# Three reorderings in a streaming-encoder block: the first weights and the residual's loads, the lag of the transposes, and where the recurrences' steps end a round

## The chip, the core and the metric

The kernel runs on one core of one Trainium2 chip. A core has a matrix engine (TensorE, "PE" in the profile), a vector engine (VectorE, DVE), a scalar engine that evaluates functions (ScalarE, ACT), GpSimd (POOL), and a queue on SyncE (SP) that issues the loads and stores in this kernel. Each engine runs its own instruction stream in order and waits on semaphores for the others. Matrix products accumulate in PSUM, of which this kernel uses eight banks (128 partitions by 512 fp32 numbers); everything else lives in SBUF.

The metric is the device time of one execution, in microseconds (us), as the median over several runs. The profile is of one execution.

## The reference

The reference is one layer of a streaming encoder on x of 256 tokens by 2048 features, in fp32, with a fixed memory of 256 tokens:

```python
x = x + 0.5 * swiglu(rms_norm(x, ffn1_norm), w_up1, w_down1)      # D_FF = 5632
h = rms_norm(x, mix_norm)
q, f, v, g, x_b, gate_b, gates = split(h @ w_in)
y_a = hgrn2(q, f, v) -> rms_norm -> * silu(g)                     # 8 heads of 128
y_b = causal conv(4) on x_b -> RG-LRU scan -> * gelu(gate_b)      # 8 blocks of 128
gt = sigmoid(gates + b_gate)
x = x + (gt[0] * (y_a @ w_branch_a) + gt[1] * (y_b @ w_branch_b)) @ w_out
x = x + cross_attention(rms_norm(x), rms_norm(mem))               # 4 heads
x = x + 0.5 * swiglu(rms_norm(x, ffn2_norm), w_up2, w_down2)
return rms_norm(x, final_norm)
```

In HGRN2 the state of a head is updated by S = diag(f) S + (1 - f) v^T; the kernel computes it through decayed scores between tokens. In RG-LRU the gates r and i are sigmoids of small block-diagonal products of the convolved input, and a linear recurrence runs over the tokens.

## The kernel before

**Weights and splits.** All weights are streamed once, in pieces of 1 MB (128 partitions x 2048). Each large fp32 product is computed as three products of a shorter type: every operand is split into h (an ACT copy, L147) and l = raw - h (a DVE subtraction, L148), and PE computes h*xh, l*xh and h*xl (`three`, L424 to L426). So ahead of each piece stand a load on SP, an ACT instruction and a DVE instruction. `weights` (L191) hands out the next piece and keeps `ahead` at two pieces: it issues the load and the split of a later piece whenever one is taken. `raw`, `h` and `l` have three buffers each.

**FFN pieces.** The two FFNs have 22 groups of 256 hidden features (gate and up) with four pieces each, and 11 blocks of the down projection with four pieces each. Twelve of the groups are "fast": two-by-two blocks multiplied with seven products in place of eight, at 42 matmuls of 256 columns a piece; their weights need sums `td` on DVE and their inputs sums `xs` (L413). A piece of an "up" group or of the down projection is 24 matmuls of 512 columns. `ffn_order` (L43) writes out the order of the pieces in Python: it spreads the fast pieces evenly from index `begin` on, and puts in the pieces of two down blocks at a time once four groups are ready for them. It counts a group ready from `seen`, the number of groups that had ended one step earlier. FFN1 has `begin` 7, FFN2 has 3.

**From a group to its transpose.** When a group's fourth piece is through, `activate` computes hid = (up * rstd) * silu(gate * rstd), 128 tokens at a time: sg on ACT (L449), hid on DVE (L450). For a fast group the sums `c` and `ev` (L496 to L504) come first. `hid` has two buffers. PE must then transpose hid (four transposes, L458, in `turn`), and ACT and DVE split the result into `hidop` (L462, L463), which the down projection reads. To keep PE from waiting for hid, `turn` is put on a list `late` with a count of 2, and `tick`, called after each piece, issues it when the count has run out, so two pieces later in the program. The tile scheduler then sets the final order on each engine, near the program's.

**The head.** FFN1 begins while nothing is loaded. For its first pieces the order of SP, ACT and DVE is the program's own, under a `manual_schedule` that closes when the fifth piece (i = 4) has been prepared. `head` is a list of things to do just before the load of piece i: the transposed x in four parts (`head_x`, pieces 0 to 3), then `head_residual` (L555, ahead of piece 4): the second part of `vt`, which holds the identity for the transposes, and the eight loads of x in token layout, with the squares for the RMS norm (`junk`, L350), and then `head_fast` (L562) for the sums of the fast pieces, ahead of pieces 5 and 6. The norm's scale rstd needs all squares; its square root (L357) and the first Silu (L449) each need their own activation table on ACT.

**The mixer's rounds.** In the mixer each unit (one or four weight pieces of a projection) is followed by `pump(2)` (L621), which takes two steps of the generators in `side`: `hgrn(hf)` (L701) or `lru(hf)` (L787), each for half of the heads. A step ends at a `yield`. In this way the recurrences' small matmuls, the ACT and the DVE work run between the projections' matmuls. The steps touched here:

- At the end of the scores in `hgrn`, four products go to PSUM and ACT copies them to `S` (L762). The next step multiplies `S` by v for two heads (L771, L772) and squares the result on ACT (`osq`, L775); the one after it sums the squares with `ones` on PE (L780) and takes the square root.
- `lru` convolves one block of 128 channels after another (xc: L803 on ACT, three L805 on DVE), with a `yield` behind the first and third of those three, and then has two products with the gates' weights (L811) and two sigmoids (L812). So the products of one block stand in the same step as the beginning of the next block's convolution.

Of the kernel before, what the change touches and what calls it, by code (L numbers as in the profile page):

```python
# [10 lines left out]
ACT = mybir.ActivationFunctionType  # L11
ALU = mybir.AluOpType

P = 128
# [29 lines left out]
def ffn_order(fast, begin):  # L44

    left = {"fast": fast, "up": NU - fast}
    begun = {"fast": None, "up": None}  # L50
    out, ended, down = [], [], []
    names = count()
    blocks = seen = 0

    def step(kind):
        if begun[kind] is None:
            begun[kind] = [next(names), 0]
            left[kind] -= 1
        g, i = begun[kind]
        out.append((kind, g, i))  # L60
        begun[kind] = [g, i + 1]
        if i == 3:
            ended.append(g)
            begun[kind] = None

    total = 4 * (NU + NB)
    while len(out) < total:
        fasts = sum(e[0] == "fast" for e in out)
        more = left["fast"] or begun["fast"]
        if more and fasts * (total - begin - 9) < 4 * fast * (len(out) - begin):  # L70
            step("fast")
            continue
        if not down and not begun["up"]:
            ready = seen // 2 - blocks
            if ready >= 2 or (ready and not left["up"] and not more):
                n = min(2, ready)
                down = [("down", blocks, n, c, b) for c in range(4) for b in range(blocks, blocks + n)]
                blocks += n
        seen = len(ended)
        if down:  # L80
            out.append(down.pop(0))
        elif left["up"] or begun["up"]:
            step("up")
        elif more:
            step("fast")
    number = {g: i for i, g in enumerate(ended)}
    return [(e[0], number[e[1]], e[2]) if e[0] != "down" else e for e in out]
# [3 lines left out]
def block_kernel(ctx: ExitStack, tc: tile.TileContext, xT, xin, memT, vec, gfin, bgate, lruw, wu1, wd1, win, wv,  # L91
# [60 lines left out]


    plan, ahead = [], []
    orders = {"ffn1": ffn_order(FAST, 7), "ffn2": ffn_order(FAST, 3)}

    def plan_ffn(name, wu, wd):
        for e in orders[name]:
# [25 lines left out]
            plan_rows(name, w, g)  # L184
    plan_ffn("ffn2", wu2, wd2)

    head = []
    planned = count()
    in_turn = ExitStack()

    def weights(*key):  # L191
        while plan and len(ahead) < 2:
            i = next(planned)
            k, src, fast = plan.pop(0)
            if i == 0:
                in_turn.enter_context(tc.manual_schedule(engines={sp.engine, act.engine, dve.engine}))
            inner = head[i]() if i < len(head) else None
            ahead.append((k, prepare(src, fast, 4 if i < 4 else 1, inner)))
            if i == 4:
                in_turn.close()  # L200
        k, w = ahead.pop(0)
        assert k == key, (k, key)
        return w
# [229 lines left out]
    def ffn(name, pairs, sq, then, begin=()):  # L433
# [7 lines left out]
        def activate(g, gate, up):  # L441

            nonlocal rstd
            if rstd is None:
                rstd = sq.rstd_tokens()
            hid = scoped["hd"].tile([P, 512], F32, name="hid", tag="hd")
            for t in range(2):
                sg = t1("sg")
                act.activation(sg, gate[t], ACT.Silu, scale=rstd[:, t:t + 1])  # L449
                dve.scalar_tensor_tensor(out=hid[:, t * T:(t + 1) * T], in0=up[t], scalar=rstd[:, t:t + 1], in1=sg,  # L450
                                         op0=ALU.mult, op1=ALU.mult)
            late.append((2, lambda: turn(g, hid)))

        def turn(g, hid):
            acc = bank()
            for z in range(2):
# [7 lines left out]
            hids[g] = o  # L464

        def tick(flush=False):
            for i in range(len(late)):
                n, f = late.pop(0)
                if n > 1 and not flush:
                    late.append((n - 1, f))  # L470
                else:
                    f()

        for e in orders[name]:
# [31 lines left out]
            elif kind == "up":  # L506
                g, piece = e[1:]
                if piece == 0:
                    accs[g] = [bank(), bank()]
                for k in range(4):  # L510
                    a = pairs[2 * piece + k // 2]
                    for t in range(2):
                        three(accs[g][t], a, w, k % 2 * T + t * P, k * 512, 512, piece + k == 0, piece + k == 6)
                if piece == 3:
                    activate(g, [b[:, T:] for b in accs[g]], [b[:, :T] for b in accs[g]])
            else:
                first, n, c, block = e[1:]
                if block == first:
                    accs["down"] = [bank(), bank()]
                for k in range(4):  # L520
                    o = hids[2 * block + k // 2]
                    a = o[:, k % 2 * 512:][:, :512]
                    for t in range(2):
                        three(accs["down"][t], (a[:, :T], a[:, T:]), w, t * P, k * 512, 512,
                              block == first and k == 0, block == first + n - 1 and k == 3)
                if block == first + n - 1:
                    for t in range(2):
                        o = xt[c][:, t * 512:(t + 1) * 512]
                        dve.scalar_tensor_tensor(out=o, in0=accs["down"][t], scalar=0.5, in1=o, op0=ALU.mult,
                                                 op1=ALU.add)  # L530
                    if block == NB - 1:
                        then(c)
# [19 lines left out]
        part(0)  # L552
        return (lambda: part(512)) if q == 0 else None

    def head_residual():  # L555
        sp.dma_start(vt[:, small_n:NVEC], vec[:, small_n:])
        for c in range(4):
            for t in range(2):
                sp.dma_start(xt[c][:, t * 512:(t + 1) * 512], xin[t * P:(t + 1) * P, c * 512:(c + 1) * 512])
            sq1.add(c)  # L560

    def head_fast(i):  # L562
        for f in fast1[2 * i:2 * i + 2]:
            f()

    head += [lambda q=q: head_x(q) for q in range(4)] + [head_residual] + [lambda i=i: head_fast(i) for i in range(2)]


    par = const.tile([P, 96], F32, name="par")
# [52 lines left out]
    def pump(n):  # L622
        while n > 0 and side:
            try:
                next(side[0])
                n -= 1
            except StopIteration:
                side.pop(0)

# [71 lines left out]
    def hgrn(hf):  # L701
# [58 lines left out]
        for h in range(4):  # L760
            pe.matmul(acc[:, h * P:(h + 1) * P], kv[:, h, :P], qv[:, h, P:], start=True, stop=True)
        act.activation(S[:, 1024:], acc, ACT.Copy)  # L762
        yield
        y = Y["a", hf] = slot(name="ya")
        for pair in range(2):
            os, squares = [], []
# [28 lines left out]
    def lru(hf):  # L795
        xb = heads(XB[hf])
        xc, r, i, a = slot(name="xc"), slot(name="r"), slot(name="i"), slot(name="a")
        lw = slot(name="lw")
        sp.dma_start(lw, lruw[:, hf * 1024:(hf + 1) * 1024])
        for n in range(4):  # L800
            b = hf * 4 + n
            o = heads(xc)[:, n]
            act.activation(o, xb[:, n], ACT.Identity, bias=col("conv_b", b), scale=col("conv_w", b))  # L803
            for j in range(1, 4):
                dve.scalar_tensor_tensor(out=o[:, j:], in0=xb[:, n, :T - j], scalar=col("conv_w", j * 8 + b),  # L805
                                         in1=o[:, j:], op0=ALU.mult, op1=ALU.add)
                if j % 2:
                    yield
            for to, wi, bias in ((r, 0, "ba"), (i, 4, "bx")):
                acc = bank()  # L810
                pe.matmul(acc[:, :T], lw[:, (wi + n) * P:(wi + n + 1) * P], o, start=True, stop=True)  # L811
                act.activation(heads(to)[:, n], acc[:, :T], ACT.Sigmoid, bias=col(bias, b))  # L812
        for n in range(4):
            b = hf * 4 + n
            act.activation(heads(a)[:, n], heads(r)[:, n], ACT.Exp, scale=c8[:, b:b + 1])
            act.activation(heads(r)[:, n], heads(r)[:, n], ACT.Tanh, scale=nc8[:, b:b + 1])

        m = slot(name="m")
        act.activation(m, a, ACT.Square)
        dve.scalar_tensor_tensor(out=m, in0=m, scalar=1.0, in1=r, op0=ALU.add, op1=ALU.mult)  # L820
        yield
        act.activation(m, m, ACT.Sqrt)
        dve.memset(heads(m)[:, :, 0:1], 1.0)
        dve.memset(heads(a)[:, :, 0:1], 0.0)
        dve.tensor_tensor(out=xc, in0=xc, in1=i, op=ALU.mult)
        yield
        dve.tensor_tensor(out=xc, in0=xc, in1=m, op=ALU.mult)
        yield
        dve.tensor_tensor_scan(out=r, data0=a, data1=xc, initial=0.0, op0=ALU.mult, op1=ALU.add)
        yield  # L830
        yield
        y = Y["b", hf] = slot(name="yb")
        act.activation(GB[hf], GB[hf], ACT.Gelu_apprx_tanh)
        dve.tensor_tensor(out=y, in0=r, in1=GB[hf], op=ALU.mult)
        yield
# [286 lines left out]
```

## Time and profile before

| what | value |
|---|---|
| runs | 2539.37, 2538.70, 2537.59 us; median 2538.7 |
| profiled execution | 2537.01 us |
| its span | 2535.2 us |
| PE busy | 2493.0 us, 98% of the span |
| DVE busy | 1890.0 us, 75% |
| ACT busy | 1319.2 us, 52% |
| DMA | 476.42 MB, 188 GB/s on average |
| mean granted clock of PE | 0.996 |

The span is from the first to the last recorded instruction; the execution's time is somewhat longer. Rows give the start in us from the span's beginning, or the busy time of a group of instructions with the mean of one in ns. "idle before <-X" names what ended an engine's idle time. The row of a wait gives the total, the times and the longest. A matmul's recorded duration overlaps the next one's, so two of them start closer together than their durations say. `L424` is line 424 of the kernel; in the changed kernel the lines lie a few further down. PSUM accumulators are all called `acc`; `ops` and `sum` are operands of the mixer's products.

### The profile page before, as it was taken

To read this page: it belongs to the slowest core of one execution; us is meant where nothing else is said; L and a number is where in the kernel's file an instruction comes from. 1 tells how busy PE (TensorE), PEld (TensorE's weight loads), DVE (VectorE), ACT (ScalarE), POOL (GpSimd) and SP (SyncE) were. 2 spreads that over 40 slices of the span, in tenths; PEclk is the share of its full clock that TensorE was granted. 3 is DMA by queue.
4 is the path that set the end of the run, shared out by engine and by line. 5 is a ranking of instruction groups with operands and counts; after the bars stand their busy time and mean duration, and the time that the engine had idled before them with its cause. 6 is when DMAs were issued, how large, how long until landed. Compare 5 with 4: busy or idle time off the path is not lost.

```text
span 2535.2 us, 33273 instructions
## 1 busy us (share of the span) xinstructions
PE 2493.0 (98%) x13730; PEld 2159.2 (85%) x13730; DVE 1890.0 (75%) x2061; ACT 1319.2 (52%) x1459; POOL 0.2 (0%) x4
## 2 busy tenths in 40 slices
PE   8999999999999999989999999999999999999998
PEld 7888888888888888878888888888888888888886
DVE  7888888888865767665565676556788888888885
ACT  7555555554554443466434554445655555555553
POOL 0000000000000000000000000000000000000000
PEclk9999999999999999999999999999999999999999
DMA  7555555555545444445555565544455555555554
GB/s 270 196 187 199 184 198 191 192 198 187 212 167 199 166 150 164 169 166 200 195 185 183 191 210 184 180 166 151 167 197 200 193 189 202 194 196 199 197 191 151
DMA packets 70279, 476.42 MB, mean 188 GB/s; under 512 B 7792, under 2 KB 8048, under 8 KB 14320
## 3 DMA queue, kind: packets, MB, share of 16 engines
q1 hardware_dynamic: 70128, 474.30, 52.6%
q8 instruction: 107, 1.75, 0.3%
q14 instruction: 44, 0.36, 0.0%
HBM read 472.17 MB, written 2.10 MB: 187 GB/s over the span
## 4 chain that ended last, share of the span: by engine, by line
PE 88%; DVE 4%; issue 3%; DMA 3%; ACT 2%; SPq 0%; DVEq 0%; ACTq 0%
PE acc L426 15%; PE acc L424 15%; PE acc L425 15%; PE acc L239 11%; PE acc L252 7%; PE acc L251 7%; PE acc L253 7%; PE acc L240 5%; DVE l L148 3%; DMA raw<-wu 3%; ACT h L147 2%; PE acc L458 1%; PE acc L739 1%; PE acc L379 1%; PE acc L811 0%
## 5 line engine op out<-in xcount | busy, mean ns | idle before, releaser
L148 DVE TENSOR_TENSOR l<-raw,h 128x2048 fp32r<-128x2048 f32 (+2 forms) x548 | 968.1, 1774 | 420.4 <-ACT h L147 419.4
L147 ACT ACTIVATE h<-raw 128x2048 fp32r<-128x2048 f32 (+2 forms) x548 | 822.0, 1502 | 816.6 <-PE acc L425 297.6
L424 PE MATMUL acc<-h,xh 128*128 128x256 f32 (+1 forms) x1984 | 633.0, 319 | 7.0 <-ACT h L147 6.9
L426 PE MATMUL acc<-l,xh 128*128 128x256 f32 (+1 forms) x1984 | 631.1, 319 | 1.5 <-DVE l L148 1.5
L425 PE MATMUL acc<-h,xl 128*128 128x256 f32 (+1 forms) x1984 | 630.7, 318 | 0.0
L424 PEld LDWEIGHTS acc<-h,xh 128*128 128x128 f32 x1984 | 378.5, 191 | 35.0 <-ACT h L147 8.7
L239 PE MATMUL acc<-ops,h 128*128 128x512 f32 x1152 | 406.3, 397 | 1.3 <-DVE ops L290 1.3
L426 PEld LDWEIGHTS acc<-l,xh 128*128 128x128 f32 x1984 | 377.8, 190 | 30.0 <-DVE l L148 4.6
L425 PEld LDWEIGHTS acc<-h,xl 128*128 128x128 f32 x1984 | 378.4, 191 | 26.4
L251 PE MATMUL acc<-h,ops 128*128 128x512 f32 x832 | 327.8, 394 | 0.0
L252 PE MATMUL acc<-h,ops 128*128 128x512 f32 x832 | 325.0, 391 | 0.7 <-DVE ops L287 0.7
L253 PE MATMUL acc<-l,ops 128*128 128x512 f32 x832 | 324.8, 390 | 0.0
L240 PE MATMUL acc<-ops,l 128*128 128x256 f32 x1152 | 321.8, 280 | 0.0
L426 PE MATMUL acc<-l,hidop 128*128 128x512 f32 x704 | 275.8, 392 | 1.7 <-DVE l L148 1.7
L424 PE MATMUL acc<-h,hidop 128*128 128x512 f32 x704 | 276.0, 392 | 0.0
L147 ACT ACTIVATE h<-td 128x1024 fp32r<-128x1024 f32 x192 | 199.5, 1049 | 145.7 <-DVE td L223 145.7
L425 PE MATMUL acc<-h,hidop 128*128 128x512 f32 x704 | 275.0, 391 | 0.0
L239 PEld LDWEIGHTS acc<-ops,h 128*128 128x128 f32 x1152 | 216.1, 188 | 52.0 <-DVE ops L290 1.8
L148 DVE TENSOR_TENSOR l<-td,h 128x1024 fp32r<-128x1024 f32 x192 | 233.0, 1220 | 23.0 <-ACT h L147 22.5
L240 PEld LDWEIGHTS acc<-ops,l 128*128 128x128 f32 x1152 | 217.3, 189 | 0.3
L252 PEld LDWEIGHTS acc<-h,ops 128*128 128x128 f32 x832 | 156.7, 188 | 32.9 <-DVE ops L287 1.1
L253 PEld LDWEIGHTS acc<-l,ops 128*128 128x128 f32 x832 | 156.5, 188 | 32.9
(203 smaller groups left out, 1952.5 us busy)
## 6 DMA issues: line engine op xcount, KB each, us to landing
raw<-wu SPq DMA_DIRECT2D x172, 1024.0 KB, 4.8
raw<-wd SPq DMA_DIRECT2D x88, 1024.0 KB, 4.8
raw<-win SPq DMA_DIRECT2D x40, 1024.0 KB, 4.8
raw<-wg SPq DMA_DIRECT2D x32, 1024.0 KB, 4.8
raw<-wab SPq DMA_DIRECT2D x16, 1024.0 KB, 4.8
raw<-wout SPq DMA_DIRECT2D x16, 1024.0 KB, 4.8
raw<-wq SPq DMA_DIRECT2D x16, 1024.0 KB, 4.8
raw<-wk SPq DMA_DIRECT2D x16, 1024.0 KB, 4.8
```

Of the source, the lines that this page charges most:

```text
L147: act.activation(h, raw, ACT.Copy)
L148: dve.tensor_tensor(out=l, in0=raw, in1=h.bitcast(F32), op=ALU.subtract)
L239: pe.matmul(acc, h[:, k * P:(k + 1) * P], xs[k], start=k == 0, stop=False)
L240: pe.matmul(acc[:, :T], l[:, k * P:(k + 1) * P], xs[k][:, :T], start=False, stop=k == KT - 1)
L251: pe.matmul(accs[t], a, hj, start=first and j == 0, stop=False)
L252: pe.matmul(accs[t], b, hj, start=False, stop=False)
L253: pe.matmul(accs[t], a, lj, start=False, stop=last and j == 3)
L379: pe.transpose(accs[m // 2][:, m % 2 * T + t * P:][:, :P], tile[:, t * 512 + m * P:][:, :P], ident)
L424: first = pe.matmul(acc, ah, bh, start=start, stop=False)
L425: pe.matmul(acc, al, bh, start=False, stop=False)
L426: return first, pe.matmul(acc, ah, bl, start=False, stop=stop)
L458: pe.transpose(acc[:, z * T + t * P:][:, :P], hid[:, t * T + z * P:][:, :P], ident)
```

## The change

The change has three parts, and no product, load or function is added or taken away.

1. **Head.** The loads of x in token layout with their squares, and the second part of `vt`, move from ahead of weight piece 4 to behind it: x0 and x1 behind piece 4, x2, x3 and `vt` behind piece 5. The sums of the fast pieces move behind pieces 6 and 7. The manual order closes at i = 5. FFN1's first fast piece comes one later (`begin` 8). The `activate` of FFN1's first group is issued three pieces later.
2. **Transposes.** `turn` has a count of 3 in place of 2, and is put on the list before hid is made; `ffn_order` takes the number of ended groups from three steps back. This changes the order of the pieces in FFN1 from the first down pieces on, and in the middle of FFN2. Where the list is flushed, all of it is issued first.
3. **Rounds.** A step may end its round: `yield True` takes the rest of the round's steps. `hgrn` does so behind the copy of `S`. `lru` convolves its four blocks first, a step each, ends the round, and then has all eight products and sigmoids in one step.

```diff
-    blocks = seen = 0
+    blocks, seen = 0, [0, 0, 0]
...
-            ready = seen // 2 - blocks
+            ready = seen[-3] // 2 - blocks
...
-        seen = len(ended)
+        seen.append(len(ended))
...
-    orders = {"ffn1": ffn_order(FAST, 7), "ffn2": ffn_order(FAST, 3)}
+    orders = {"ffn1": ffn_order(FAST, 8), "ffn2": ffn_order(FAST, 3)}
...
-            if i == 4:
+            if i in rest:
+                rest[i]()
+            if i == 5:
                 in_turn.close()
...
+            late.append((3, lambda: turn(g, hid)))
             hid = scoped["hd"].tile([P, 512], F32, name="hid", tag="hd")
...
-            late.append((2, lambda: turn(g, hid)))
...
         def tick(flush=False):
+            while late and flush:
+                late.pop(0)[1]()
             for i in range(len(late)):
                 n, f = late.pop(0)
-                if n > 1 and not flush:
+                if n > 1:
...
-                    activate(g, [b[:, T:] for b in accs[g]], [b[:, :T] for b in accs[g]])
+                    gate, up = ([b[:, a:a + T] for b in accs[g]] for a in (T, 0))
+                    if rest and g == 0 and name == "ffn1":
+                        late.append((3, lambda g=g, gate=gate, up=up: activate(g, gate, up)))
+                    else:
+                        activate(g, gate, up)
...
-    def head_residual():
-        sp.dma_start(vt[:, small_n:NVEC], vec[:, small_n:])
-        for c in range(4):
+    def head_residual(i):
+        for c in (2 * i, 2 * i + 1):
             for t in range(2):
                 sp.dma_start(xt[c][:, t * 512:(t + 1) * 512], xin[t * P:(t + 1) * P, c * 512:(c + 1) * 512])
             sq1.add(c)
+        if i:
+            sp.dma_start(vt[:, small_n:NVEC], vec[:, small_n:])
...
-    head += [lambda q=q: head_x(q) for q in range(4)] + [head_residual] + [lambda i=i: head_fast(i) for i in range(2)]
+    head += [lambda q=q: head_x(q) for q in range(4)]
+    for i in range(2):
+        rest[4 + i] = lambda i=i: head_residual(i)
+        rest[6 + i] = lambda i=i: head_fast(i)
...
-                next(side[0])
-                n -= 1
+                n -= n if next(side[0]) else 1
...
         act.activation(S[:, 1024:], acc, ACT.Copy)
-        yield
+        yield True
...
-                if j % 2:
-                    yield
-            for to, wi, bias in ((r, 0, "ba"), (i, 4, "bx")):
+            yield
+        yield True
+        for to, wi, bias in ((r, 0, "ba"), (i, 4, "bx")):
+            for n in range(4):
                 acc = bank()
-                pe.matmul(acc[:, :T], lw[:, (wi + n) * P:(wi + n + 1) * P], o, start=True, stop=True)
-                act.activation(heads(to)[:, n], acc[:, :T], ACT.Sigmoid, bias=col(bias, b))
+                pe.matmul(acc[:, :T], lw[:, (wi + n) * P:(wi + n + 1) * P], heads(xc)[:, n], start=True, stop=True)
+                act.activation(heads(to)[:, n], acc[:, :T], ACT.Sigmoid, bias=col(bias, hf * 4 + n))
```

More of the change, by code (lines that the diff above doesn't have):

```diff
@@ L185, in block_kernel @@
     plan_ffn("ffn2", wu2, wd2)
-    head = []
+    head, rest = [], {}
     planned = count()
```

## The prediction, made before the changed kernel had run

> **What bounds the kernel now.** I read the busy line first, then PE's waits (engine and line that waited, releaser, sum in us, times, longest), then stretches around each large wait.
>
> ```profile
> PE 2493.0 (98%) x13730; PEld 2159.2 (85%) x13730; DVE 1890.0 (75%) x2061; ACT 1319.2 (52%) x1459; POOL 0.2 (0%) x4
> ```
>
> ```profile
> PE acc L811 <- DVE xc L805: 6.9, 1, 6.9
> PE acc L424 <- ACT h L147: 6.9, 3, 5.7
> PE acc L458 <- DVE hid L450: 6.5, 7, 1.4
> PE acc L771 <- ACT S L762: 3.6, 2, 1.8
> PE acc L426 <- DVE l L148: 3.1, 9, 0.5
> ```
>
> TensorE (PE) is busy 98% of the span and the change takes no matmul away: the order of instructions has as many matmuls and transposes on PE in both kernels. So only PE's stalls can move the time, and the first four rows are the places that the diff touches: the head (L147), the transposes (L458), the end of a step of hgrn (L771) and lru's convolution (L811). Now what each costs, as stretches of the span (window; busy us of PE, PEld, DVE, ACT and POOL; granted clock; DMA share; GB/s):
>
> ```profile
> 20.00:31.00 11.00, 10.82 (x48) 8.63 (x46) 9.63 (x27) 10.69 (x27) 0.00 (x0) 1.00 1.04 393
> 31.00:36.55 5.55, 0.00 (x0) 0.00 (x1) 2.29 (x6) 5.50 (x10) 0.00 (x0) 0.72 0.62 255
> 36.55:41.00 4.45, 4.20 (x10) 2.89 (x11) 3.58 (x4) 4.44 (x5) 0.00 (x0) 0.58 0.24 53
> 929.50:931.40 1.90, 0.10 (x2) 0.09 (x1) 0.86 (x1) 1.76 (x3) 0.00 (x0) 1.00 0.96 405
> 1120.60:1127.50 6.90, 0.00 (x0) 0.02 (x1) 6.87 (x9) 5.41 (x7) 0.00 (x0) 0.87 0.75 274
> 1127.50:1134.00 6.50, 6.49 (x18) 5.22 (x19) 3.63 (x9) 3.86 (x6) 0.00 (x0) 0.61 0.24 100
> 300.00:400.00 100.00, 100.00 (x600) 89.26 (x599) 85.97 (x87) 53.32 (x53) 0.00 (x0) 1.00 0.55 200
> ```
>
> The two long stalls are paid twice: behind each PE is busy at a lower granted clock, and a stretch at clock c loses (1-c) of itself. Head: 4.45 x 0.42 = 1.9. lru: 6.50 x 0.39 = 2.5. After the 1.80 us stall at 929.5 the clock stays 1.00.
>
> One turn, with a matmul ahead of it (the timeline of PE, DVE and ACT):
>
> ```profile
> 108.87 0.39 PE L425 MATMUL acc<-h,xl 128*128 128x512 f32 x1
> 109.10 0.39 PE L426 MATMUL acc<-l,xh 128*128 128x512 f32 x1
> 110.30 0.30 PE L458 MATMUL acc<-vt,hid 128*128 128x128 f32 x1 [0.82 <-DVE hid L450]
> 109.68 0.88 DVE L450 SCALAR_TENSOR_TENSOR hid<-ev,rtok,sg 128x256 f32<-128x256 f32 x2
> 102.89 0.38 ACT L496 ACTIVATE c<-acc 128x256 f32<-128x256 f32 x1
> ```
>
> Matmuls start 0.23 apart, here 1.20: 0.97 lost where the list says 0.82. I add this 0.15 to every stall. Before: head 5.7 + 1.9 + 0.15 and 0.25 of the L426 row (the l of weight 4) = **8.0**; turns 6.5 + 7 x 0.15 = **7.55**; hgrn 3.6 + 0.3 = **3.9**; lru 6.9 + 2.5 + 0.15 = **9.6**. That is 29.0 us that the change can win at most here.
>
> **Part 1, the head: gain 4.9.** The residual's eight loads (2.1 MB, 5.3 us at 393 GB/s) stood ahead of weight 4; now four (x0, x1) stand behind weight 4 and four, with the second part of vt, behind weight 5. No DMA is added. When weight 3's last quarter landed, and what ACT and DVE take here:
>
> ```profile
> L214 SPq DMA_DIRECT2D raw<-wu x1: 328/328/328, 15.9 to 15.9; - x1
> DMA to landing us min/median/max: 6.0/6.0/6.0
> ```
>
> ```profile
> 25.65 0.61 ACT L350 ACTIVATE junk<-x 128x512 f32<-128x512 f32 x1
> ...
> 27.83 0.63 ACT L147 ACTIVATE xh<-xs 128x512 fp32r<-128x512 f32 x1 [0.25 <-DVE xs L413]
> ...
> 32.59 1.28 ACT L357 ACT_TABLE_LOAD   x1
> 33.88 0.30 ACT L357 ACTIVATE stdt<-stdt,eps 128x2 f32<-128x2 f32 x1
> ...
> 34.60 1.89 ACT L147 ACTIVATE h<-raw 128x2048 fp32r<-128x2048 f32 x1
> ```
>
> ```profile
> 26.70 0.49 DVE L413 TENSOR_TENSOR xs<-xg 128x128 f32<-128x128 f32 x2
> 27.11 0.28 DVE L413 TENSOR_TENSOR xs<-xs,xg 128x128 f32<-128x128 f32 x1
> ...
> 36.53 2.29 DVE L148 TENSOR_TENSOR l<-raw,h 128x2048 fp32r<-128x2048 f32 x1 [1.11 <-ACT h L147]
> ```
>
> Weight 4 follows weight 3 (landed 15.9 + 6.0 = 21.9) and lands 1.05 MB / 393 GB/s = 2.7 later, at 24.6, so ACT splits it as soon as weight 3's quarters are done, 25.65 to 27.55 instead of from 34.60. DVE has 12 sums (0.2 apart by the rows, from 26.7 on) ahead of its l: 26.7 + 12 x 0.2 + 2.3 = 31.4. PE ends weight 3 at 30.7 (busy 10.82 of the 11.00 from 20.00, less the last matmul's modelled tail of 0.16) and needs this l four products of 0.23 later, at 31.6: no wait. A piece of weights is 24 such products, 5.45. Weight 5 lands at 29.9, but by the order its split stands behind the squares of x0 and x1 and four xh: 27.55 + 4 x 0.61 + 4 x 0.53, with waits for sums among them, gives 32.8 to 34.7; its l, behind five sums and four xl, 35.6 to 37.9. PE comes at 36.1 (30.7 + 5.45) and needs that l at 37.0: **1.0 lost**. Then ACT has four squares, two xh, two table loads (1.28 each), stdt and one sg before weight 6: h at 41.25 to 43.15, l 43.2 to 45.5. PE ends weight 5 at 42.5: it waits 0.65 for h and, four products on, 1.45 for l. Weight 7 is ready at 48.1, before PE's 50.1. New stalls 3.1, none near the 5.7 behind which the clock fell; gain 8.0 - 3.1 = **4.9**. No row shows this order, so the bounds are 0.5 (the same work just stalls PE elsewhere) and 8.0 (all hidden); I take the sum of rows.
>
> [...]
>
> **Part 2, turns three pieces behind: gain 7.55.** In the seven waits a group's hid was late by at most 1.4 + 0.15. hid comes 109.68 + 0.88 = 110.56, 7.7 us after its group's last product freed c (102.89). One piece more is 24 products x 0.23 = 5.5 us (a fast piece, 42 shorter ones, 5.0), so the slack is at least 5.0 - 1.6 = 3.4 at each of them, and hid's chain has no new link. Group 0's activate, three pieces later, frees its two PSUM banks later: at most fast 4 + up or down 2 + turn 1 = 7 of 8 then stand open. hid has two buffers: its third group ends after the first has turned. What could become late next is the hidop that a down piece reads; the order of pieces uses the lag of three for that, so its first reader moves too. The new order also moves splits against PE: by the order of instructions PE follows an l closely at four places of FFN1, where it was seven. I count nothing for it; bounds 5 (each of nine waits for l, 3.1 in all, nearly doubled) and 8.
>
> **Part 3, hgrn's round ends behind S: gain 0.9.**
>
> ```profile
> 928.59 1.91 ACT L147 ACTIVATE h<-raw 128x2048 fp32r<-128x2048 f32 x1 [0.16 <-PE acc L239]
> 930.41 0.36 ACT L262 ACTIVATE lo<-acc 128x256 f32<-128x256 f32 x1
> 930.67 0.59 ACT L762 ACTIVATE S<-acc 128x512 f32<-128x512 f32 x1
> 932.27 0.38 ACT L775 ACTIVATE osq<-acc 128x256 f32<-128x256 f32 x1 [1.01 <-PE acc L772]
> 931.32 0.70 PE L771 MATMUL acc<-S,v 128*128 128x256 f32 x2 [1.80 <-ACT S L762]
> ```
>
> S stood on ACT behind the split of the next weight and lo. Now a unit's products lie between S and its reader, and both waits go (3.9). But pairs of steps shift: the squares' products (L780) now follow the output products (L771, L772) in the same round, where a unit lay between. In hgrn(0) the order has nothing between them on PE, and ACT again has the split (1.82 to its next start) and lo (0.26) first: from the unit's end T the squares (0.38) end at T + 2.65 and 3.0, the products at T + 3.5 instead of T + 2.15: **1.34 for each of two pairs**. In hgrn(1) four products lie between and 0.18 is left each. New 3.0, gain **0.9**; bounds -1.5 (hgrn(1) stalls as hgrn(0), and a split finds ACT later) and 3.9.
>
> **Part 4, lru's gates in one step: gain 9.6.**
>
> ```profile
> 1126.93 3.23 DVE L805 SCALAR_TENSOR_TENSOR xc<-plain,vt,xc 128x253 f32<-128x253 f32 x8
> L811 PE MATMUL acc<-xc,lw x32: 377/378/764, 1079.7 to 1149.7; 128*128 128x256 f32 x32
> ```
>
> DVE ran a convolution for the products of the same round, behind yb and a split. After the change each convolution has a whole unit (5 us) before its product: no wait, no half clock. Eight products then stand together on eight banks; the last two need a bank back (from the gate's addition, DVE, 0.75, or in lru(1) a sigmoid behind a 1.9 split), for which the six before give 6 x 0.38 = 2.3: 0 to 0.3. Eight sigmoids, a table load and eight exp or tanh (some 11 us of ACT) stand together as well; the next split needed comes 1 us or more before PE by the order. ACT has 10 table loads fewer (1.28 each), which PE doesn't feel, ACT being busy 52%. Gain **9.6**, bounds 6 (the clock still falls at one place) and 10.7 (the 0.2 at each of eight switches to L811 also goes for six).
>
> **Sum.** 4.9 + 7.55 + 0.9 + 9.6 = 22.95. The profiled execution took 2537.0 (span 2535.2); 2514.0 after. The runs' median, 2538.7, is 1.7 over it: **2515.7**.
>
> **Rivals.**
> (1) The head's stall only moves: splits 5 and 6 stand behind squares and table loads, and x's landings push ACT by the 5 us that weight 4 gains. Then Part 1 is 0: 2520.6. For it: ACT is busy 10.69 of 11.00 from 20 to 31. Against: PE has 5.45 us of weight 4 to do meanwhile, which it hadn't.
> (2) The turns' evacuation now meets the splits of the next piece, and PE waits for l instead. Each turn has a hidop of 0.68 on DVE:
>
> ```profile
> L463 DVE TENSOR_TENSOR hidop<-acc,hidop 128x512 fp32r<-128x512 f32 x44 | 30.1, 684 | 1.9 <-ACT hidop L462 1.9
> ```
>
> If a quarter of it shows, 7.5 us are lost and Part 2 is nothing: 2523.2. It decides the sign from (22.95 + 5.1) / 44 = 0.64 a turn; with all 0.68 it costs 29.9 against a gain of 22.95: **2538.7 + 6.95 = 2545.7, slower**. Against: from 300 to 400 DVE is busy 86.0 of 100 with PE at 100, and all waits for l are 3.1.
> (3) Everything is hidden, in the head and hgrn too: 3.1 + 3.0 more, 2509.6.
> [...]
> (5) The order is not what the diff says: the order of instructions shows each move, so I give it nothing.
>
> **How the numbers follow.** Forecast (2511 to 2519.5) 0.60, (1) 0.15, (2) 0.16, (3) 0.06, (4) 0.03. Of (2), half (0.08) is a loss of up to a quarter of a hidop a turn, the other half more, up to the slower end. The range, 2508 to 2524, holds all but that half and tails of the forecast. 0.2% (5.1 us) is about what a measurement of this kernel tells from no change. Within 0.2% is 0.03 of (2), slower 0.05 of it; faster is the rest, 0.92.
>
> **What would show it.** In the waits after: the L811, hid and S rows gone; a row of the squares (osq) of some 2.5 in hgrn(0); in the head waits for h and l at two pieces, none over 1.5; clock 1.00 from 20 to 60 and from 1100 to 1140. Wrong would be: a stall over 3 us in the head, a clock of 0.50 beside it, or many new waits for l in FFN1.

## The result, and the profile after

| | before | after |
|---|---|---|
| median of the runs | 2538.14 us | 2515.39 us |
| profiled execution | 2537.01 us | 2516.06 us |
| its span | 2535.2 us | 2514.3 us |

The ratio of the times is 0.991, with a 95% interval of 0.9893 to 0.9928: the changed kernel is 22.75 us faster. 2515.7 was predicted. The lines of the changed kernel stand a few further down: L424 to L426 are now L426 to L428, L458 is L459, L771 is L781, L780 is L790, L811 is L822.

The busy line of the page, after:

```profile
PE 2485.7 (99%) x13730; PEld 2157.2 (86%) x13730; DVE 1889.2 (75%) x2061; ACT 1303.5 (52%) x1449; POOL 0.2 (0%) x4
```

PE has the same 13730 instructions; its busy time is 7.3 us less, in part since none of them starts in a stretch that the clock's records give as 0.50, where 19 did before (7 from 33.44 to 40.27, 12 from 1125.71 to 1132.54). ACT has the ten table loads fewer. PE's waits after (engine and line that waited, releaser, total us, times, longest):

```profile
PE acc L428 <- DVE l L148: 5.9, 9, 1.1
PE acc L426 <- ACT h L147: 5.2, 4, 2.1
PE acc L790 <- ACT osq L785: 2.3, 2, 1.2
```

The rows for the convolution (6.9), for hid (6.5) and for S (3.6) are gone, and the squares (osq) are the new row that was foretold. What is left for h is four short waits, three of them in the first 16 us, where the first loads are awaited. Stretches of the span after (window; busy us of PE, PEld, DVE, ACT, POOL; granted clock; DMA share; GB/s):

```profile
25.00:37.00 12.00, 12.00 (x55) 9.88 (x54) 12.00 (x32) 11.39 (x22) 0.00 (x0) 1.00 1.03 394
37.00:50.00 13.00, 9.81 (x41) 7.18 (x40) 10.88 (x20) 12.27 (x18) 0.00 (x0) 1.00 0.33 110
922.00:940.00 18.00, 15.66 (x87) 13.54 (x86) 12.98 (x15) 8.95 (x13) 0.00 (x0) 1.00 0.37 127
1080.00:1140.00 60.00, 60.00 (x268) 50.03 (x267) 43.16 (x42) 47.94 (x59) 0.00 (x0) 1.00 0.51 183
```

The clock is 1.00 in all of them. From 1080 to 1140, where the convolution had stalled PE, it is busy 60.00 of 60.00. The head still loses 3.2 us between 37 and 50, at these three places (the timeline of PE, with its waits):

```profile
39.12 0.73 PE L428 MATMUL acc<-l,xh 128*128 128x512 f32 x2 [0.68 <-DVE l L148]
45.33 0.50 PE L426 MATMUL acc<-h,xh 128*128 128x512 f32 x1 [1.38 <-ACT h L147]
47.66 0.73 PE L428 MATMUL acc<-l,xh 128*128 128x512 f32 x2 [1.13 <-DVE l L148]
```

**Where the time went, stage by stage.** Two matmuls after a wait that both kernels have serve as marks, the first of the mixer and one of the branch projections. Before:

```profile
746.87 0.50 PE L239 MATMUL acc<-ops,h 128*128 128x512 f32 x1 [0.65 <-DVE ops L290]
1243.74 0.50 PE L252 MATMUL acc<-h,ops 128*128 128x512 f32 x1 [0.72 <-DVE ops L287]
```

After:

```profile
735.47 0.50 PE L241 MATMUL acc<-ops,h 128*128 128x512 f32 x1 [0.65 <-DVE ops L292]
1220.82 0.50 PE L254 MATMUL acc<-h,ops 128*128 128x512 f32 x1 [0.72 <-DVE ops L289]
```

FFN1 won 746.87 - 735.47 = 11.4 (12.45 had been forecast: 4.9 + 7.55). The mixer won (1243.74 - 746.87) - (1220.82 - 735.47) = 11.5 (forecast 10.5). By the spans' difference of 20.9, 2.0 were lost again behind it, where the change does little and nothing had been forecast; 1.7 of that is told of in the last section.

### The profile page after: what moved, and what is told of

It is laid out like the page before. It is cut to its first block, busy times and chain, and to the rows that moved or that the text cites. A ratio compares the mean times of both kernels' runs of the same rounds, so it can differ in the third digit from the quotient of the medians.

```text
span 2514.3 us, 33255 instructions
## 1 busy us (share of the span) xinstructions
PE 2485.7 (99%) x13730; PEld 2157.2 (86%) x13730; DVE 1889.2 (75%) x2061; ACT 1303.5 (52%) x1449; POOL 0.2 (0%) x4
## 4 chain that ended last, share of the span: by engine, by line
PE 91%; DVE 3%; issue 2%; DMA 2%; ACT 1%; SPq 0%; DVEq 0%; ACTq 0%
PE acc L428 16%; PE acc L427 16%; PE acc L426 16%; PE acc L241 11%; PE acc L254 8%; PE acc L255 7%; PE acc L253 7%; PE acc L242 5%; DVE l L148 2%; DMA raw<-wu 1%; ACT h L147 1%; PE acc L459 1%; PE acc L749 1%; PE acc L381 1%; DMA xf<-xT 0%
## 5 line engine op out<-in xcount | busy, mean ns | idle before, releaser
L426 PE MATMUL acc<-h,xh 128*128 128x256 f32 (+1 forms) x1984 | 632.5, 319 | 5.2 <-ACT h L147 5.2
L428 PE MATMUL acc<-l,xh 128*128 128x256 f32 (+1 forms) x1984 | 629.0, 318 | 3.5 <-DVE l L148 3.5
L241 PE MATMUL acc<-ops,h 128*128 128x512 f32 x1152 | 408.0, 399 | 1.3 <-DVE ops L292 1.3
L426 PEld LDWEIGHTS acc<-h,xh 128*128 128x128 f32 x1984 | 377.8, 190 | 32.9 <-ACT h L147 6.6
L428 PEld LDWEIGHTS acc<-l,xh 128*128 128x128 f32 x1984 | 377.4, 190 | 31.6 <-DVE l L148 6.5
L242 PE MATMUL acc<-ops,l 128*128 128x256 f32 x1152 | 322.1, 280 | 0.0
L428 PE MATMUL acc<-l,hidop 128*128 128x512 f32 x704 | 274.9, 390 | 2.5 <-DVE l L148 2.5
L426 PE MATMUL acc<-h,hidop 128*128 128x512 f32 x704 | 276.0, 392 | 0.0
L241 PEld LDWEIGHTS acc<-ops,h 128*128 128x128 f32 x1152 | 216.3, 188 | 53.2 <-DVE ops L292 1.8
L242 PEld LDWEIGHTS acc<-ops,l 128*128 128x128 f32 x1152 | 217.4, 189 | 0.3
```

Of the source, the lines that this page charges most:

```text
L241: pe.matmul(acc, h[:, k * P:(k + 1) * P], xs[k], start=k == 0, stop=False)
L242: pe.matmul(acc[:, :T], l[:, k * P:(k + 1) * P], xs[k][:, :T], start=False, stop=k == KT - 1)
L426: first = pe.matmul(acc, ah, bh, start=start, stop=False)
L428: return first, pe.matmul(acc, ah, bl, start=False, stop=stop)
```

## The experiments

Each is compared with the kernel before on the same chip (before: 2538.12, 2538.06 or 2537.3 us). The diffs are shortened (`...`, and comments in place of lines): every version with a `yield True` or with lru's part also has the new line in `pump`, and both versions of the turns have the new flush in `tick`.

**The head alone.** The first part of the diff on the kernel before:

```diff
-    orders = {"ffn1": ffn_order(FAST, 7), ...
+    orders = {"ffn1": ffn_order(FAST, 8), ...
...
+            if i in rest:
+                rest[i]()          # residual behind weights 4 and 5, sums behind 6 and 7
-            if i == 4:
+            if i == 5:
                 in_turn.close()
...
+                    if rest and g == 0 and name == "ffn1":
+                        late.append((3, lambda g=g, gate=gate, up=up: activate(g, gate, up)))
...
```

> Only part 1 (weight 4 ahead of the residual's loads, begin 8, first activate three pieces later), on the kernel before. Theory: the 8.0 us of stall and half clock at 31 to 41 us give way to three short waits at pieces 5 and 6, 3 to 3.7 us in all, no half clock there: 4 to 5 us less than before, about 2533.5. Rival 1 (the stall only moves): no change, and a wait over 5 us in the first 60 us. FFN1's seven waits for hid stay near 6.5.

2533.39 us, ratio 0.9982 (0.9973 to 0.9991): 4.7 less, as forecast (4.9). In the rows the wait of 5.7 is gone and the longest for h is 1.1; hid keeps its 6.3 in seven waits:

```profile
PE acc L460 <- DVE hid L452: 6.3, 7, 1.6
...
PE acc L426 <- ACT h L147: 3.4, 4, 1.1
```

Rival 1, that the stall only moves, falls. One expectation failed in this profile: behind the short waits at piece 6 the clock was halved all the same (windows of the same kernel):

```profile
46.50:48.00 1.50, 1.03 (x3) 0.85 (x4) 1.50 (x3) 1.50 (x4) 0.00 (x0) 0.50 0.20 38
48.00:50.00 2.00, 2.00 (x6) 1.62 (x5) 2.00 (x2) 1.58 (x1) 0.00 (x0) 0.52 0.79 291
```

**Only the later activate.** The loads stay where they were:

```diff
-    orders = {"ffn1": ffn_order(FAST, 7), ...
+    orders = {"ffn1": ffn_order(FAST, 8), ...
...
-                    activate(g, [b[:, T:] for b in accs[g]], [b[:, :T] for b in accs[g]])
+                    ...                              # gate and up, as in the whole diff
+                    if g == 0 and name == "ffn1":
+                        late.append((3, lambda g=g, gate=gate, up=up: activate(g, gate, up)))
+                    else:
+                        activate(g, gate, up)
```

> On the kernel before only begin 8 and the activate of the first group three pieces later; the residual's loads stay ahead of weight 4. Theory (the place of weight 4's load and split decides): its split still stands behind eight squares and now five xh, the stall for h L147 stays at 5 to 6 us with the half clock behind it, and l comes later as all the sums stand ahead of it on DVE: no gain, 2537 to 2541. Rival (the square root and its table load ahead of the split were the cause): the stall shrinks by 2 us or more, without the half clock, 2534.

2538.16 us, ratio 1.0004 (0.9994 to 1.0013): no change. The wait shrank by 1.1 only, and one for l grew to 1.1 behind it:

```profile
36.59 0.79 PE L424 MATMUL acc<-h,xh 128*128 128x512 f32 x1 [4.61 <-ACT h L147]
39.78 1.22 PE L426 MATMUL acc<-l,xh 128*128 128x512 f32 x2 [1.11 <-DVE l L148]
```

The half clock behind it lasted 10.2 us in this profile, 6.8 before, which costs 1.7 of it again. So the square root ahead of the split was not the main cause: without it the wait is 1.1 shorter. By difference, part 1's gain comes with the rest of it, the place of the loads, of the squares that follow them and of the sums; these were not run one by one.

**The turns alone**, first with the whole of part 2, then with the count alone:

```diff
+            late.append((3, lambda: turn(g, hid)))
...
-            late.append((2, lambda: turn(g, hid)))
...                                                  # only in the first of the two:
-            ready = seen // 2 - blocks
+            ready = seen[-3] // 2 - blocks
```

> Only part 2 (turns three pieces behind, ffn_order with the lag of three), begin 7 as before. Theory: all seven waits for hid go, 7.5 us less, about 2530.5; waits for l change by under 1.5 us. Rival 2 (the turns' evacuation pushes the splits): waits for l in the FFNs grow by as much as is won, 2538 or more. The stalls in the head, at S and at the convolution stay.

> On the kernel before only the count of the turns, 3 in place of 2, with ffn_order as it was. By the order a turn still stands at least three pieces ahead of the down piece that reads its hidop. Theory (the lag of the turn alone wins part 2): no wait for hid, 7.5 us less, about 2530.5 as with the whole of part 2. Rival (the lag of three in ffn_order is needed, or does some of it): waits for hidop or more waits for l, and 2533 or more.

2529.95 us, ratio 0.9969 (0.9957 to 0.998), and 2530.12 us, ratio 0.9972 (0.9962 to 0.9983): 8.2 and 7.2 less. No row for hid is left in either. With the whole part the row for l is

```profile
PE acc L426 <- DVE l L148: 4.7, 10, 0.7
```

Waits for l grew from 3.1 to 4.7, over both FFNs; with the count alone they are 3.5. Rival 2, that the evacuation pushes the splits by as much as is won, falls. The lag of three in `ffn_order` was not needed here: the count wins it.

**The end of the round in hgrn alone, and lru's part alone:**

```diff
         act.activation(S[:, 1024:], acc, ACT.Copy)
-        yield
+        yield True
```

> Only the end of the round behind the copy of S. Theory: the two waits for S (3.6 us) go, and two waits for the squares of 1.2 us each come in the first half: 0.5 to 1.5 us less than before, about 2537, not to be told from no change by the time but by the rows. Rival: both halves wait for the squares and the time is the same or worse by 1.5.

```diff
-                if j % 2:
-                    yield
...
+            yield
+        yield True
+        for to, wi, bias in ((r, 0, "ba"), (i, 4, "bx")):
+            for n in range(4):       # eight products and sigmoids in one step
...
```

> Only part 4 (convolutions first, end of the round, eight products in one step). Theory: the 6.9 us wait and the half clock behind it go, and six of eight small losses of 0.2 at the switches to the gates' products: 9.5 to 11 us less, about 2528. A rival that prices the wait alone gives 7 (2531); one that has the wait move to the banks or the sigmoids gives under 5.

2529.69 us, ratio 0.9967 (0.9955 to 0.998), and 2529.61 us, ratio 0.9964 (0.9951 to 0.9977). lru's part won 8.5, near its forecast. hgrn's part won 8.4 where 0.9 had been forecast. Its list of waits says why:

```profile
PE acc L424 <- ACT h L147: 8.2, 4, 5.7
PE acc L458 <- DVE hid L450: 6.5, 7, 1.4
PE acc L426 <- DVE l L148: 2.4, 8, 0.6
PE acc L779 <- ACT osq L774: 2.3, 2, 1.2
```

The squares stand there with 2.3, as forecast; but the 6.9 at the convolution are gone too, though lru's code is untouched. The end of the round moves all later steps of the list `side` against the units. DVE before, and in the kernel with hgrn's part alone (its timeline):

```profile
1122.62 2.29 DVE L148 TENSOR_TENSOR l<-raw,h 128x2048 fp32r<-128x2048 f32 x1
1124.82 0.48 DVE L805 SCALAR_TENSOR_TENSOR xc<-plain,vt,xc 128x255 f32<-128x255 f32 x1
1125.22 0.75 DVE L694 SCALAR_TENSOR_TENSOR gate<-acc,rtok,bgate 128x512 f32<-128x512 f32 x1
```

```profile
1122.07 1.23 DVE L833 TENSOR_TENSOR yb<-r,plain 128x1024 f32<-128x1024 f32 x1
1123.22 1.40 DVE L693 SCALAR_TENSOR_TENSOR gate<-acc,rtok,bgate 128x512 f32<-128x512 f32 x2
1124.54 2.44 DVE L804 SCALAR_TENSOR_TENSOR xc<-plain,vt,xc 128x255 f32<-128x255 f32 x6
```

Before, the second half's convolution began behind yb and a split with its products already waiting; now it follows the gate directly and the split comes after it.

**Both mixer parts together:**

```diff
+        yield True                   # in hgrn, behind the copy of S
...
+        yield True                   # in lru, behind four convolutions; then the eight products
```

> Parts 3 and 4 together on the kernel before. Alone they won 8.4 and 8.5 us, each without the 6.9 us wait at the convolution. Theory A: they remove the same stall twice, so that together they win about 10 (2528): the rows show the squares twice at 1.2, no wait for S, none for the convolution. Theory B: they add up, 17 us, 2521.

2526.47 us, ratio 0.9958 (0.9944 to 0.9973): 11.6 less, not 17. Both remove the same stall once. Its waits show neither S nor xc, and the squares with 2.3. The three parts alone (head 4.7, turns 8.2, mixer 11.6) add up to 24.5, against 22.75 for the whole change; by their intervals these are not to be told apart.

**lru's part without its end of round** (the diff is against lru's part):

```diff
             yield
-        yield True
         for to, wi, bias in ((r, 0, "ba"), (i, 4, "bx")):
```

> Part 4 without its end of round, on the kernel before: convolutions first, a step each, and the eight products in the step right behind the last of them. Theory (a convolution needs a unit between it and its product): the fourth convolution, behind a split of 2.3 us on DVE, stalls the products for 2 to 6 us in one or both halves: 2531 to 2535. Rival (to convolve first is enough): 2529.6 as with the whole of part 4, no wait for xc.

2529.37 us, ratio 0.9965 (0.9954 to 0.9977): the same 8 us as the whole of part 4, and no wait for xc in the rows. My reason for the gain, a whole unit between a convolution and its product, falls: to convolve all four blocks first, and then to have the eight products in one step, is enough.

**A second end of round, behind the squares,** in the changed kernel:

```diff
                 squares.append(s)
-            yield
+            yield True
```

> The changed kernel with a second end of round, behind the squares. By the order the products of the squares then stand behind a unit for the second pair of the first half, and still directly behind the output products for its first pair, where the unit between is empty. Theory: one of the two waits for the squares of 1.2 goes, 1.3 us less, about 2514, and nothing new. Rival: the two rounds more that each half takes bring back a wait for the convolution or for S, 2517 to 2525.

2515.99 us, ratio 0.9915 (0.9901 to 0.993), not to be told from the changed kernel. One of the two waits for the squares went; two others came, 1.1 for a sigmoid and this one:

```profile
1031.99 1.13 PE L771 MATMUL acc<-silu,k 128*128 128x128 f32 x8 [1.48 <-DVE k L762]
```

**The manual order closed later,** in the changed kernel, by two pieces, and this edit together with the last one:

```diff
-            if i == 5:
+            if i == 7:
                 in_turn.close()
```

> The changed kernel with the manual order closed at i = 7 in place of 5. In it the split of piece 5 no longer stands behind four xh, nor that of piece 6 behind the two table loads. Theory (the head's remaining stalls are ACT's order): the waits at pieces 5 and 6 of 0.8, 1.5 and 1.3 go, 3 to 4 us less than the changed kernel's 2515.4, about 2512. Rival (ACT has too much to do there whatever its order): the waits come at pieces 6 to 8 instead and the time is 2515.

> The last two edits together on the changed kernel. Theory: 4 to 5.5 us less than the changed kernel, about 2510.5, faster than both kernels; one wait for the squares is left in the rows, and none over 0.5 for h or l between 25 and 60 us.

2520.51 us, ratio 0.9932 (0.9916 to 0.9949), and 2521.39 us, ratio 0.9935 (0.992 to 0.995): 5 us slower than the changed kernel (the intervals just overlap, but all eight runs of the two took 2518.9 or more, and the changed kernel's four at most 2516.1). The waits at pieces 5 and 6 did go, but a single one came at piece 7:

```profile
56.12 0.79 PE L426 MATMUL acc<-h,xh 128*128 128x512 f32 x1 [8.60 <-ACT h L147]
```

ACT could not reach that piece's split earlier because the order written by the program puts four xh ahead of it, each behind its own sums on DVE, and then the two table loads (ACT's timeline of the kernel closed at 7):

```profile
42.08 0.63 ACT L147 ACTIVATE xh<-xs 128x512 fp32r<-128x512 f32 x1 [3.29 <-DVE xs L415]
44.41 0.63 ACT L147 ACTIVATE xh<-xs 128x512 fp32r<-128x512 f32 x1 [1.69 <-DVE xs L415]
...
49.88 0.63 ACT L147 ACTIVATE xh<-xs 128x512 fp32r<-128x512 f32 x1 [2.51 <-DVE xs L415]
```

**Closed one piece later, with the fast pieces beginning two later:**

```diff
-    orders = {"ffn1": ffn_order(FAST, 8), ...
+    orders = {"ffn1": ffn_order(FAST, 10), ...
-            if i == 5:
+            if i == 6:
                 in_turn.close()
```

> The changed kernel with the manual order closed at i = 6 and begin 10: by the order the four xh and the sums stand behind piece 6's split, and the first fast piece, which needs them, comes two pieces later than with begin 8. Theory (what the head lacks is room between the sums and their first reader): the waits at pieces 5 and 6 shrink to under 1 us in sum, a wait of up to 2 us for l at the piece ahead of the first fast one: 1 to 3 us less than the changed kernel, about 2513.5. Rival (the stall moves on, as with the order closed at i = 7): a stall over 4 us, 2518 or more.

2510.89 us, ratio 0.99 (0.9884 to 0.9917). From 25 us on the head is free of stalls:

```profile
25.00:37.00 12.00, 12.00 (x55) 9.94 (x54) 7.59 (x9) 11.72 (x24) 0.00 (x0) 1.00 1.03 400
37.00:50.00 13.00, 13.00 (x59) 10.78 (x58) 9.82 (x15) 9.97 (x8) 0.00 (x0) 1.00 0.59 221
50.00:60.00 10.00, 10.00 (x48) 8.30 (x47) 9.69 (x29) 6.80 (x10) 0.00 (x0) 1.00 0.61 231
```

Its median is 4.5 below the changed kernel's, from two comparisons whose intervals overlap, and one of its four runs took 2515.0. That the three waits went, 3.2 us of them, is shown by the rows. Of the 5.1 us between the two profiles another 1.7 come from the query products of the last section, which this edit doesn't touch. So that the version beats the changed kernel is likely, and by how much is not shown.

## Why the prediction was right, point by point

**The bound.** PE's waits were the right list to go by: the 5.7 in the head and the rows for hid, S and the convolution went. Of the 29.0 that stood in them, less 3.6 in the head and 2.6 for the squares that took their place (each with its 0.15), 22.8 are left; the medians differ by 22.75 and the two profiles by 20.95 (see "The sum").

**Part 1, 4.9 forecast, 4.7 measured alone.** The three waits came at the two pieces named, none over 1.5: 1.0, 0.65 and 1.45 were foretold, and by the list and its 0.15 they were 0.8, 1.5 and 1.3. The second was mis-sized: ACT stood idle for rtok between the two table loads ahead of that split, which the working had left out (ACT's timeline, after):

```profile
38.91 1.28 ACT L359 ACT_TABLE_LOAD   x1
40.20 0.29 ACT L359 ACTIVATE stdt<-stdt,eps 128x2 f32<-128x2 f32 x1
...
41.71 1.28 ACT L452 ACT_TABLE_LOAD   x1 [0.69 <-DVE rtok L361]
```

The step "none near the 5.7 behind which the clock fell" held in the profile after, but it is not a rule: in the head alone the clock fell behind waits that were as short (0.95 and 1.13). The bound for that was missing, some 1.7 us.

**Part 2, 7.55 forecast, 8.2 measured alone.** The gain is right, as all seven waits went, but the slack behind it is not. The step "the slack is at least 5.0 - 1.6 = 3.4 at each of them" supposed that hid ends as early as before, since "hid's chain has no new link". In the changed kernel six of the 44 turns start 0.4 us after hid's end, and two of them did so with part 2 alone. At this one a split stands on DVE between hid's two halves (the timeline of DVE and PE, after):

```profile
215.12 0.48 DVE L453 SCALAR_TENSOR_TENSOR hid<-ev,rtok,sg 128x256 f32<-128x256 f32 x1
217.15 2.29 DVE L148 TENSOR_TENSOR l<-raw,h 128x2048 fp32r<-128x2048 f32 x1 [1.55 <-ACT h L147]
219.36 0.48 DVE L453 SCALAR_TENSOR_TENSOR hid<-ev,rtok,sg 128x256 f32<-128x256 f32 x1
220.22 0.60 PE L459 MATMUL acc<-vt,hid 128*128 128x128 f32 x4
```

No wait came of it, by 0.4 us; that part of Part 2 was luck. The sentence that the lag in `ffn_order` keeps hidop's reader back was not needed. "I count nothing" for the l splits was off by 1.6 us in the part alone (waits for l 4.7 for 3.1); in the changed kernel they are 5.9, of which 1.8 stand in the head and were counted in Part 1.

**Parts 3 and 4, 0.9 and 9.6 forecast, 11.6 measured together.** The new waits for the squares came out as worked out in the first half: 1.34 for each of two pairs forecast, and by the rows 1.17 and the 0.15 that the list leaves out. The 0.18 for each pair of the second half left no row:

```profile
926.17 1.13 PE L790 MATMUL acc<-osq,ones 128*128 128x256 f32 x4 [1.17 <-ACT osq L785]
935.33 1.13 PE L790 MATMUL acc<-osq,ones 128*128 128x256 f32 x4 [1.17 <-ACT osq L785]
```

What failed is the attribution. "Part 3 ... gain 0.9" and "Part 4 ... gain 9.6" added up right only because each stall was counted once; alone, Part 3 is worth 8.4. I had looked at hgrn's own waits only, and not at what the end of its round does to every later step. And Part 4's "a whole unit before its product" is not what it took. The 1.1 by which the two parts exceed 10.5 is near the upper bound that I gave for Part 4 (10.7: six of the eight switches to the gates' products fall away) and inside the intervals.

**The sum.** For the profiled execution 2514.0 was forecast and 2516.06 came. The median's 0.3 of difference is better than the working was: the misses on both sides (mixer +1.0, FFN1 -1.05, -2.0 behind the mixer) came to -2.05 in the profile, and the profile after lay 0.7 over its median where the one before lay 1.1 under its own. Of FFN1's shortfall, 1.1 lies ahead of every changed instruction, in the wait for a load at the start, 0.96 before and 2.05 after, which the other profiles show at 1 to 2 as well:

```profile
14.20 0.50 PE L424 MATMUL acc<-h,xh 128*128 128x512 f32 x1 [0.96 <-ACT h L147]
```

```profile
15.43 0.50 PE L426 MATMUL acc<-h,xh 128*128 128x512 f32 x1 [2.05 <-ACT h L147]
```

**The rivals.** (1) and (2) fell by the parts alone. (3) did not come: 3.2 in the head and 2.3 for the squares stayed. (4), given 0.03, has no run behind it: ACT's table load of 1.28 at 38.91 is followed at 40.20, 1.29 later, just as the one at 32.59 was followed at 33.88 before.

## What to carry to other kernels

Where an engine is busy 98%, list its waits, price each from its own stage with the slower clock behind it, and ask of every one what takes its place; here that came to within 1.1 us for each of the two stages, FFN1 and the mixer, though not for each part of the change. Gains of parts that move the same steps don't add: a step that ends a round early shifts everything behind it, so work out each part's effect on the later steps too, not on its own wait alone. And a written order that removes one wait can put an engine's next job behind a slower one: closing the manual order two pieces later cost 5 us, one piece later, with the fast pieces beginning two pieces later, cleared the head from 25 us on.

## What the runs showed of the hardware that was not expected

**The clock can fall behind a short stall.** Behind the stalls of 5.7 and 6.9 us in the kernel before, PE's granted clock was 0.50; behind those of 4.6 (only the later activate) and 8.6 (the order closed at 7) a matmul took 0.63 us in place of 0.39. But in lru's part alone the clock fell behind the same 1.8 us wait for S that left it at 1.00 in the kernel before. In the clock's records of the kernel before, the times from one change to the next are 27.31 us at 1.00, 6.83 at 0.50, 1085.44 at 1.00, 6.83 at 0.50 and 1396.05 at 1.00, and after the change 2501.97 at 1.00; that is 8, 2, 318, 2, 409 and 733 steps of 3.41 us. In lru's part alone the whole stall lies within one stretch of that length, and the half clock is the next one (windows of that kernel):

```profile
929.11:932.52 3.41, 1.61 (x13) 1.38 (x12) 1.42 (x2) 2.98 (x4) 0.00 (x0) 1.00 0.90 308
932.52:935.93 3.41, 3.41 (x12) 2.86 (x12) 2.17 (x4) 1.07 (x3) 0.00 (x0) 0.50 0.22 62
```

That cost 3.41 x 0.50 = 1.7 us. In the kernel before, by the same steps (busy by the modelled ends of the matmuls), PE was busy for 0.79 us of the 3.41 ahead of the first half clock and for none of those ahead of the second, and for 1.78 and 1.66 us of the steps with the two waits for S (the first runs 0.2 over its step), behind which the clock stayed at 1.00. What decides at such a short stall is open, for in the whole of part 2 alone the same stall lay within one step too, with the same 1.61 us busy as in lru's part, and the clock stayed:

```profile
922.02:925.43 3.41, 1.61 (x11) 1.35 (x10) 1.76 (x2) 2.40 (x4) 0.00 (x0) 1.00 0.63 259
```

So the same stall of 1.8 us was free in one profile and cost 1.7 us in another.

**The same products run at two speeds.** The cross-attention's query products are 89 us of nothing but L239 and L240 (L241 and L242 after), at clock 1.00 and with PE always busy. Before, and after, in windows of 89 us from the same product on:

```profile
1431.00:1520.00 89.00, 89.00 (x515) 78.45 (x515) 65.41 (x96) 51.45 (x80) 0.00 (x0) 1.00 0.58 207
```

```profile
1408.08:1497.08 89.00, 89.00 (x505) 77.23 (x505) 63.80 (x93) 51.55 (x80) 0.00 (x0) 1.00 0.56 204
```

These are 515 matmuls against 505. From the first start to the last of the 518 in this stretch it took 89.9 us in nine of the profiles and 91.6 in five (the changed kernel, the head alone, only the later activate, the whole of part 2, both mixer parts), nothing between. No part of the change sets it, as all of them are also in the four variants of the changed kernel, which had 89.9. The key products behind them, by the same two lines, took 84.8 us in all 14 profiles, 0.354 us a pair, which is the slower of the two speeds. The query products are 1.7 of the 2.0 us that the changed kernel's profile lost behind the mixer. What sets the speed is open.
